# Opening in two half pieces with an identity made on the chip, and a last step that goes by token tiles

## The chip, the cores and the metric

The kernel runs on one core of a Trainium2 chip. The metric is device time in microseconds (us) of one execution; lower is better. TensorE is PE, VectorE is DVE, ScalarE is ACT, GpSimd is POOL, and SyncE (SP) issues most of the DMAs.

## The reference

One layer of a hybrid encoder in fp32, for one sequence of 256 tokens and a width of 2048:

```python
h = rms_norm(x, attn_norm[layer])
x = x + hybrid_mixer(h, w_in[layer], b_forget[layer], q_norm[layer], k_norm[layer],
                     out_norm_fox[layer], out_norm_sb[layer], w_out[layer])
h = rms_norm(x, ffn_norm[layer])
x = x + conv_ffn(h, w_up[layer], conv_w[layer], conv_b[layer], w_down[layer])
```

`hybrid_mixer` projects `h` with `w_in` (2048 x 6152) to queries, keys and values of 8 heads of forgetting attention, 8 forget gates, and queries, keys and values of 8 heads of stick-breaking attention; both results are normalized and go through `w_out` (2048 x 2048). `conv_ffn` is `w_up` (2048 x 11264), a causal convolution of width 3 per column, a SiLU gate, and `w_down` (5632 x 2048).

## The kernel before

The 256 tokens are two tiles of 128 (`NT`), the width is 16 tiles of 128 (`KT`). Nearly all of the time is products of the activations with the four weight matrices. Each weight is read once from DRAM, in pieces of up to 1 MB. For accuracy in fp32 each operand is split into a high and a low part: `split` (L238) lets ACT round a piece to `w_hi` (L242) and DVE subtract it from the raw piece to `w_lo` (L243), and `in_three` (L252) sums high x high, low x high and high x low in PSUM. The activations stand transposed in `hT` as a high and a low part.

The work is a list of steps, one per piece of weights. Each step has a load, perhaps a sum, a preparation (the split), products, and perhaps a follow-up. The loop at the end (L1242) writes them out staggered: step n's load stands six steps ahead of its products, its split two steps ahead. Every engine then runs its own instructions strictly in the order written. Loads go into five buffers in turn (`wraw`, L80), so a load waits until the piece five steps back has been split; high and low parts have three buffers each. SP issues the loads in order; some additions to weights and a reload of `x` go by POOL's DMA queue, for the first time long after the opening.

`opening` (L317) takes the first 688 columns of the values of `w_in`, for all 16 tiles of the width, in eight pieces of two tiles each (2 x 688 columns, 688 KB). `tokens` of a piece transposes two tiles of `x` on PE with an identity (`transposed`, L169, into `ps_x`), multiplies them by the norm's weight `ga` into `hT`, high part on ACT (L181) and low part on DVE (L182), and splits the piece. `matmuls` of a piece are 24 products of 128x344 into four banks `acc_v`; after them PE does the transposes of the piece two steps on. `ga` is a column form of `attn_norm`, which arrives as 16 rows in `prow` and is turned by a transpose of its own (`columns`, L164, into `pp`). The identity is the first 128 columns of `cst`, an input array of constants, and comes by DMA into `cs` (L327).

The order of SP's first transfers is: x tiles 0 and 1, identity, `attn_norm`, x tiles 2 and 3, weights 0, x tiles 4 and 5, weights 1, and so on. All other parameters are loaded behind the seventh piece (`load_parameters`, L138).

After the opening come the other projections (several with seven products instead of eight per block of four), the heads of attention in between, `w_out`, and the feed-forward. The last eight steps are `down_plain` (L1149) with `final` set: for each 512 output columns two pieces of 4 x 512 weights, 24 products of 128x512 each into the two halves of one tile `acc`, one half per token tile. Products of the two token tiles alternate. Then `added` (L1083) adds each half to `xb` on DVE (L1085) and sends it to `out` by SP (L1087).

Of the kernel before, what the change touches and what calls it, by code (L numbers as in the profile page):

```python
# [7 lines left out]

F32 = mybir.dt.float32
F32R = mybir.dt.float32r  # L10
AF = mybir.ActivationFunctionType
ALU = mybir.AluOpType
# [31 lines left out]
def hybrid_layer(  # L44
# [18 lines left out]
):  # L63
    nc = tc.nc
    act, dve = nc.scalar, nc.vector
    act.preload_act_table_set("natural_log_exp_and_others")

    xf = x.rearrange("b s d -> (b s) d")
    of = out.rearrange("b s d -> (b s) d")
# [20 lines left out]


    NC2 = 2 * NFT
    cs = const.tile([P, C_MF], F32, name="cs")
    prow = const.tile([50, P], F32, name="prow")
# [19 lines left out]
    def load_x(k, n, queue=nc.sync):  # L114
        queue.dma_start(x2[:, :, k * P : (k + n) * P], xp[:, :, k * P : (k + n) * P])

    ident = cs[:, C_ID : C_ID + P]
    tri = cs[:, C_TRI : C_TRI + P]
    tri_one = cs[:, C_TRI : C_TRI + 2 * P]
    ones = cs[:, C_ONE : C_ONE + P]  # L120
# [48 lines left out]
    def transposed(k):  # L169
        ps = psb.tile([P, 2, S], F32, name="ps_x", tag="t")  # L170
        for j in range(2):
            for t in range(NT):
                nc.tensor.transpose(  # L173
                    ps[:, j, t * P : (t + 1) * P], x2[:, t, (k + j) * P : (k + j + 1) * P], ident
                )
        return ps

    def split_tokens(ps, k, g):
        for j in range(2):
            i = k + j  # L180
            act.activation(hT[:, i, 0, :], ps[:, j, :], AF.Identity, scale=g[:, i : i + 1])  # L181
            dve.scalar_tensor_tensor(  # L182
                hT[:, i, 1, :], ps[:, j, :], g[:, i : i + 1], f32(hT[:, i, 0, :]),
                op0=ALU.mult, op1=ALU.subtract,
            )
# [19 lines left out]
    def new_step(load, sums, prepare, matmuls, follow=None):  # L205
        steps.append((load, sums, prepare, matmuls, follow))
# [31 lines left out]
    def split(raw, a, b):  # L238
        hi = whi.tile([P, 2048], F32R, name="w_hi", tag="w_hi")
        lo = wlo.tile([P, 2048], F32R, name="w_lo", tag="w_lo")  # L240
        n = a * b
        act.copy(hi[:, :n], raw[:, :n])  # L242
        dve.tensor_tensor(lo[:, :n], raw[:, :n], f32(hi[:, :n]), op=ALU.subtract)  # L243
# [8 lines left out]
    def in_three(accs, parts, n, lhs, starts, stops, cut=None, middle=None):  # L252

        hi, lo = parts
        order = [(i, l, hi) for i in range(n) for l in range(2)] + [(i, 0, lo) for i in range(n)]
        for j, (i, l, r) in enumerate(order):
            if middle and 2 * j == len(order):
                middle()
            for t, o in enumerate(accs):
                nc.tensor.matmul(  # L260
                    o, lhs(i, l, t), r[:, i, :] if cut is None else r[:, i, cut], start=starts and j == 0,
                    stop=stops and j == 3 * n - 1, skip_group_check=len(accs) == 1 and not starts,
                )

    def middle():
# [51 lines left out]
    def opening():  # L317

        banks = []
        x_loads = {0: [(4, 2)], 1: [(6, 2)], 2: [(8, 4)], 3: [(12, 4)]}  # L320
        mem = {}

        def piece(i):
            def loads():
                if i == 0:
                    load_x(0, 2)
                    nc.sync.dma_start(cs[:, :P], cst[:, :P])  # L327
                    nc.sync.dma_start(prow[:KT, :], attn_norm[0].rearrange("(n p) -> n p", p=P))
                    load_x(2, 2)
                mem["raw", i] = load(rows_of(wi, 2 * i, 2, V0, 2 * VC))  # L330
                for k, n in x_loads.get(i, ()):
                    load_x(k, n)
                if i == 6:
                    load_parameters()

            def tokens():
# [5 lines left out]
                if i % 2:  # L342
                    squares(ss1, i // 2)
                if i == 7:
                    ready.add("x")

            def matmuls():
                if i == 0:
                    banks.extend([bank_tile(f"acc_v{t}", 2 * j + t) for t in range(NT)] for j in range(2))
                for j in range(2):  # L350
                    in_three(
                        [banks[j][t][:, :VC] for t in range(NT)], mem["parts", i], 2, of_tokens(2 * i),
                        i == 0, i == 7, cut=slice(j * VC, (j + 1) * VC),
                    )
                if i + 2 < 8:
                    tokens_of[i + 2]()

            tokens_of.append(tokens)

            def follow():  # L360
                v = tile_of["v"] = at.tile([P, NT, WF], F32, name="vA", tag="v")
                for j in range(2):
                    for t in range(NT):
                        act.activation(
                            v[:, t, j * VC : (j + 1) * VC], banks[j][t][:, :VC], AF.Identity,
                            scale=rstd1[:, t : t + 1],
                        )
                    yield

            new_step(loads, None, tokens if i < 2 else None, matmuls, follow if i == 7 else None)  # L370

        tokens_of = []
        for i in range(8):
            piece(i)

    opening()


    def last_values():
# [703 lines left out]
    def added(c, ps, t, op=ALU.add, final=False):  # L1083
        xs = x2[:, t, c : c + 512]
        dve.tensor_tensor(xs, xs, ps, op=op)  # L1085
        if final:
            nc.sync.dma_start(of[t * P : (t + 1) * P, c : c + 512], xs)  # L1087
        yield
# [60 lines left out]
    def down_plain(part, c, final=False):  # L1149
        n = (part.f_hi - part.f_lo) // 4  # L1150
        cell = []

        def piece(kh):
            mem = {}

            def loads():
                mem["raw"] = load(rows_of(wd, part.f_lo + 4 * kh, 4, c, 512))

            def prepare():
                mem["parts"] = split(mem["raw"], 4, 512)  # L1160

            def matmuls():
                if kh == 0 and final:
# [4 lines left out]
                in_three(  # L1168
                    cell, mem["parts"], 4,
                    lambda i, p, t: of_half(part.pairs[2 * kh + i // 2][:, :, i % 2], p, t),  # L1170
                    kh == 0, kh == n - 1,
                )
# [56 lines left out]
    def begin(task):  # L1229
        next(task)  # L1230
        after.append(task)

    hooks[5] = lambda: following.append(factors1())
    hooks[7] = head_parameters
    hooks[13] = lambda: begin(token_sums())
# [82 lines left out]
```

## Time and profile before

| | us |
|---|---|
| median of three runs | 1116.45 (1116.01 to 1116.59) |
| the profiled execution, its own time | 1116.26 |
| span of the program in it (first to last instruction) | 1114.5 |
| PE busy | 1100.6 |
| DVE busy | 898.6 |
| ACT busy | 730.7 |
| first product of the opening starts | 10.36 |
| last product starts its row | 1107.46, with 8 products in 1.98 |

Times in the profile count from the start of the span. A row of the timeline has start and length in us, the engine, the line, the operation, what it writes and reads, shape and count, and in brackets how long the engine had been idle and what ended that. A row of a chain has start, length and name only. `xN` merges N instructions; lengths of products overlap, so N of them last less than N lengths. In groups, the numbers behind the bar are busy us and mean ns of one. Rows on DMAs have the count, KB each and the median us from issue to landing; POOLq and SPq are the queues of those who issue. The granted TensorE clock is 1.000 over the span.

### The profile page before, as it was taken

How to read it: one execution, taken by the hardware profiler on the slowest of the kernel's cores; microseconds unless marked ns; L12 is line 12 of the kernel's file. 1: busy time of each engine (PE TensorE's matmuls, PEld its weight loads, DVE VectorE, ACT ScalarE, POOL GpSimd, SP SyncE). 2: the span in 40 equal slices, each digit the busy share in tenths (PEclk: the TensorE clock that was granted, in tenths of full speed). 3: DMA queues.
4: the chain of work that ended last, by engine and by line, in shares of the span. 5: the costliest groups of instructions: out<-in, count | busy, mean ns of one | idle time of the engine just before them, and what ended most of it. 6: DMA issues, size and time to landing. Idle time of an engine off the chain costs nothing.

```text
span 1114.5 us, 14460 instructions
## 1 busy us (share of the span) xinstructions
PE 1100.6 (99%) x5730; PEld 948.7 (85%) x5730; DVE 898.6 (81%) x854; ACT 730.7 (66%) x915; POOL 36.6 (3%) x34
## 2 busy tenths in 40 slices
PE   7999999999999999999999999999999999999998
PEld 6988888888888888888888888888888888888886
DVE  4676888877897676666699898989899898999882
ACT  5645787667676467666676767776677666776751
POOL 0000000000100000000000000000000000000000
PEclk9999999999999999999999999999999999999999
DMA  8757877769778366555558796697958798597841
GB/s 290 268 197 209 242 189 249 184 199 259 262 174 281 114 197 200 191 190 192 190 150 242 233 262 228 189 283 197 276 182 213 261 239 274 152 289 202 265 159 66
DMA packets 166813, 240.75 MB, mean 216 GB/s; under 512 B 4168, under 2 KB 98010, under 8 KB 166746
## 3 DMA queue, kind: packets, MB, share of 16 engines
q1 hardware_dynamic: 152442, 210.47, 56.2%
q0 software_dynamic: 14304, 29.36, 15.0%
q8 instruction: 45, 0.74, 0.3%
q14 instruction: 22, 0.18, 0.0%
HBM read 237.72 MB, written 2.10 MB: 215 GB/s over the span
## 4 chain that ended last, share of the span: by engine, by line
PE 95%; DVE 2%; ACT 1%; issue 1%; DMA 1%; SPq 0%; DVEq 0%; ACTq 0%
PE pu L1069 44%; PE bank_a L260 16%; PE bank_b L260 8%; PE acc_o L260 5%; PE bank_c L260 4%; PE acc_v L260 4%; PE acc L260 4%; PE bank_p L260 4%; PE bank_e L260 2%; DVE w_lo L243 1%; ACT w_hi L242 1%; DMA w_raw<-in_w_in_dram 1%; PE ps_x L173 1%; PE ps_h L605 0%; PE ps_s L686 0%
## 5 line engine op out<-in xcount | busy, mean ns | idle before, releaser
L243 DVE TENSOR_TENSOR w_lo<-w_raw,w_hi 128x2048 fp32r<-128x2048 f32 (+1 forms) x239 | 537.2, 2252 | 146.1 <-ACT w_hi L242 145.5
L242 ACT CAST w_hi<-w_raw 128x2048 fp32r<-128x2048 f32 (+1 forms) x239 | 449.2, 1881 | 232.0 <-PE pu L1069 87.4
L1069 PE MATMUL pu<-hT,w_hi 128*128 128x512 f32 x1408 | 334.7, 390 | 0.0
L1069 PEld LDWEIGHTS pu<-hT,w_hi 128*128 128x128 f32 x1408 | 262.4, 188 | 53.4 <-DVE hT L182 0.3
L1069 PEld LDWEIGHTS pu<-hT,w_lo 128*128 128x128 f32 x1408 | 180.6, 191 | 6.9
L1069 PE MATMUL pu<-hT,w_lo 128*128 128x256 f32 x1408 | 182.8, 283 | 0.0
L999 ACT ACTIVATE tap<-up,ccol 128x256 f32<-128x256 f32 x176 | 74.6, 495 | 0.0
L260 PE MATMUL bank_a<-w_hi,g 128*128 128x512 f32 x192 | 47.3, 392 | 0.0
L1112 POOL DMA_DIRECT2D w_raw<-in_w_down_dram x16 | 20.5, 1282 | 687.9 <-DVE w_raw L1130 362.0
L260 PE MATMUL bank_a<-w_hi,hT 128*128 128x512 f32 x160 | 40.6, 396 | 0.0
L260 PEld LDWEIGHTS bank_a<-w_hi,g 128*128 128x128 f32 x192 | 34.8, 189 | 6.4
L260 PE MATMUL acc_v<-w_hi,hT 128*128 128x344 f32 x192 | 35.6, 333 | 2.9 <-ACT w_hi L242 2.9
L1130 DVE TENSOR_TENSOR w_raw<-w_raw 128x2048 f32<-128x2048 f32 x16 | 36.6, 2286 | 0.1
L260 PEld LDWEIGHTS acc_v<-w_hi,hT 128*128 128x128 f32 x192 | 31.9, 196 | 3.4 <-ACT w_hi L242 3.3
L260 PEld LDWEIGHTS bank_a<-w_hi,hT 128*128 128x128 f32 x160 | 29.2, 188 | 5.6
L1004 DVE TENSOR_TENSOR gate<-gate,tap 128x512 f32<-128x512 f32 x44 | 30.3, 688 | 2.7 <-DVE gate L1004 0.5
L1085 DVE TENSOR_TENSOR xb<-xb,bank_a 128x512 f32<-128x512 f32 x40 | 27.2, 680 | 6.2 <-PE bank_a L260 6.2
L1004 DVE TENSOR_TENSOR val<-val,tap 128x512 f32<-128x512 f32 x44 | 30.3, 688 | 2.3
L260 PE MATMUL bank_a<-w_hi,s 128*128 128x512 f32 x128 | 32.1, 392 | 0.0
L260 PE MATMUL bank_b<-w_hi,s 128*128 128x512 f32 x128 | 32.0, 392 | 0.0
L985 DVE TENSOR_TENSOR up<-t,R 128x512 f32<-128x512 f32 x44 | 30.4, 692 | 1.5
L260 PE MATMUL acc_o<-w_hi,oSb 128*128 128x512 f32 x128 | 31.3, 396 | 0.0
(273 smaller groups left out, 1410.7 us busy)
## 6 DMA issues: line engine op xcount, KB each, us to landing
w_raw<-in_w_up_dram SPq DMA_DIRECT2D x88, 1024.0 KB, 5.3
w_raw<-in_w_down_dram SPq DMA_DIRECT2D x44, 1024.0 KB, 5.2
w_raw<-in_w_in_dram SPq DMA_DIRECT2D x40, 1024.0 KB, 5.7
w_raw<-in_w_out_dram SPq DMA_DIRECT2D x16, 1024.0 KB, 6.3
w_raw<-in_w_down_dram POOLq DMA_DIRECT2D x16, 1024.0 KB, 8.9
w_raw<-in_w_in_dram SPq DMA_DIRECT2D x12, 688.0 KB, 8.1
w_raw<-in_w_in_dram POOLq DMA_DIRECT2D x8, 1024.0 KB, 9.7
xb<-in_x_dram POOLq DMA_DIRECT2D x4, 512.0 KB, 8.1
```

What stands on the lines that cost most here:

```text
L173: nc.tensor.transpose(ps[:, j, t * P : (t + 1) * P], x2[:, t, (k + j) * P : (k + j + 1) * P], ident)
L242: act.copy(hi[:, :n], raw[:, :n])
L243: dve.tensor_tensor(lo[:, :n], raw[:, :n], f32(hi[:, :n]), op=ALU.subtract)
L260: nc.tensor.matmul(o, lhs(i, l, t), r[:, i, :] if cut is None else r[:, i, cut], start=starts and j == 0, stop=stops and j == 3 * n - 1, s ...
L985: dve.tensor_tensor(u[:, :, 2:], t2, R, op=ALU.mult)
L999: act.activation(taps[w][:, j, :], u[:, j, w : w + S], AF.Copy, scale=ccol[:, w, f : f + 1])
L1004: dve.tensor_tensor(a, a, tap, op=ALU.add)
L1069: nc.tensor.matmul(acc[:, j, S:] if low else acc[:, j, :], (lo if low else hi)[:, i, j * P : (j + 1) * P], hT[:, k, 0, :] if low else hT[: ...
L1085: dve.tensor_tensor(xs, xs, ps, op=op)
L1112: nc.gpsimd.dma_start(mem[weights].rearrange("p (a b) -> p a b", a=4), plus, accum_op=ALU.add)
L1130: dve.tensor_tensor(mem[into], mem[a], mem[b], op=ALU.add)
```

## The change

It changes the two ends of the program and no product in between.

The opening has nine pieces, the first two of one tile each (344 KB). Piece 0 is rounded by DVE instead of ACT, and its products go high x high for all four banks, low x high, then high x low. Tiles 0 and 1 are transposed together ahead of piece 0, and the transposes of tiles 2 and 3 now stand between the products of piece 0 and piece 1; before, they stood ahead of all products. `attn_norm` is loaded by ACT's queue, ahead of ACT's table load. The identity is not loaded: `make_identity` has POOL write zeros and select ones on the diagonal. SP's order becomes x 0-1, weights 0, weights 1, x 2-3, weights 2, x 4-5, and so on. The hooks that follow the opening are counted from its end, so they keep their place.

The last step, which is the last 4 x 512 weights of the last 512 columns, goes by token tiles: 12 products of tile 0, its addition and transfer, 12 products of tile 1, whose addition and transfer are cut into two halves of 256 columns, one sent by SP and one by ACT. The two accumulators of these 512 columns are banks of their own.

```diff
-    act.preload_act_table_set("natural_log_exp_and_others")
...
+    prow = const.tile([50, P], F32, name="prow")
+    act.dma_start(prow[:KT, :], attn_norm[0].rearrange("(n p) -> n p", p=P))
+    act.preload_act_table_set("natural_log_exp_and_others")
...
     ident = cs[:, C_ID : C_ID + P]
+    make_identity(nc, ident)
...
-        x_loads = {0: [(4, 2)], 1: [(6, 2)], 2: [(8, 4)], 3: [(12, 4)]}
+        sizes = [1, 1] + [2] * 7
+        starts = [sum(sizes[:i]) for i in range(len(sizes))]
+        last = len(sizes) - 1
+        x_loads = {0: (0, 2), 1: (2, 2), 2: (4, 2), 3: (6, 2), 4: (8, 4), 5: (12, 4)}
...
             def loads():
                 if i == 0:
-                    load_x(0, 2)
-                    nc.sync.dma_start(cs[:, :P], cst[:, :P])
-                    nc.sync.dma_start(prow[:KT, :], attn_norm[0].rearrange("(n p) -> n p", p=P))
-                    load_x(2, 2)
-                mem["raw", i] = load(rows_of(wi, 2 * i, 2, V0, 2 * VC))
-                for k, n in x_loads.get(i, ()):
-                    load_x(k, n)
-                if i == 6:
+                    load_x(*x_loads[i])
+                mem["raw", i] = load(rows_of(wi, k0, n, V0, 2 * VC))
+                if 0 < i < 6:
+                    load_x(*x_loads[i])
+                if i == 7:
                     load_parameters()
 
             def tokens():
-                ps = transposed(2 * i)
-                if i == 0:
+                if n == 1 and i == 0:
                     columns(ga, prow[:KT, :], KT)
-                split_tokens(ps, 2 * i, ga)
-                mem["parts", i] = split(mem["raw", i], 2, 2 * VC)
+                    ps = mem["ps"] = transposed(0)
+                    hi, lo = cast(mem["raw", 0], 2 * VC, dve.tensor_copy)
+                    split_tokens(ps, 0, ga, 1)
+                    mem["parts", 0] = subtracted(mem["raw", 0], hi, lo, 1, 2 * VC)
+                elif n == 1:
+                    split_tokens(mem["ps"], 0, ga, 1, 1)
+                    mem["parts", 1] = split(mem["raw", 1], 1, 2 * VC)
+                else:
+                    split_tokens(transposed(k0), k0, ga)
+                    mem["parts", i] = split(mem["raw", i], 2, 2 * VC)
...
+                if final and kh == n - 1 and c == D - 512:
+                    for t in range(NT):
+                        in_three([cell[t]], mem["parts"], 4, lambda i, p, _: lhs(i, p, t), kh == 0, True, group=True)
+                        if t < NT - 1:
+                            for _ in added(c, cell[t], t, final=True):
+                                pass
...
             def follow():
+                if final and c == D - 512:
+                    for h, queue in enumerate((nc.sync, act)):
+                        cut = slice(h * 256, (h + 1) * 256)
+                        xs = x2[:, NT - 1, c + h * 256 : c + (h + 1) * 256]
+                        dve.tensor_tensor(xs, xs, cell[NT - 1][:, cut], op=ALU.add)
+                        queue.dma_start(of[(NT - 1) * P :, c + h * 256 : c + (h + 1) * 256], xs)
+                    return
```

How the instructions stand on the engines shows three places. The first is POOL, from the start of the program. Before, its own work begins with a DMA (the first row of weights is far behind the opening):

```order
L1303 ISA
L1303 MEMSET const-float32-0.0 128x1
L1303 MEMSET const-float32-1.0 128x1
L1303 MEMSET const-bfloat16-1.0 128x1
L1303 MEMSET const-uint8-127 128x1
L1313 UNCONDITIONAL_BRANCH
L489 DMA w_raw<-in_w_in_dram 128x4x512 x8
```

With the change, `cs` being the constants' tile whose first 128 columns are the identity:

```order
L1345 MEMSET const-uint8-127 128x1
L1355 UNCONDITIONAL_BRANCH
masks.py:197 MEMSET cs 128x128
masks.py:199 ISA
masks.py:199 AFFINE_SELECT cs<-cs 128x128
L518 DMA w_raw<-in_w_in_dram 128x4x512 x8
```

Three instructions are new ahead of POOL's first DMA. [...]

The second place is PE at the start, before:

```order
L173 MATMUL ps_x<-cs,xa 128x128 x4
L166 MATMUL pp<-cs,prow 128x16
L173 MATMUL ps_x<-cs,xa 128x128 x4
L260 MATMUL acc_v_184<-w_hi,hT 128x344
L260 MATMUL acc_v_185<-w_hi,hT 128x344
```

and with the change, where L373 are the products of a half piece and `acc_v_168` to `acc_v_171` the four banks:

```order
L169 MATMUL pp<-cs,prow 128x16
L176 MATMUL ps_x<-cs,xa 128x128 x4
L373 MATMUL acc_v_168<-w_hi,hT 128x344
L373 MATMUL acc_v_169<-w_hi,hT 128x344
...
L373 MATMUL acc_v_171<-w_lo,hT 128x344
L176 MATMUL ps_x<-cs,xa 128x128 x4
L373 MATMUL acc_v_168<-w_hi,hT 128x344
```

The transpose of `prow` (`pp`) moved to the front, where it is what waits for the identity; the second four transposes moved from ahead of all products to behind the first twelve. On DVE the rows `COPY ga<-pp` and then `CAST w_hi<-w_raw 128x688` are the first two with the change.

The third place is PE at the end. `bank_a_8927` and `bank_a_8928` are the accumulators of token tiles 0 and 1 in the changed kernel, the two names with `g2` the activations:

```order
L269 MATMUL bank_a_8927<-w_hi_8923,g2_8526 128x512 x4
L269 MATMUL bank_a_8927<-w_hi_8923,g2_8782 128x512 x4
L269 MATMUL bank_a_8927<-w_lo_8924,g2_8526 128x512 x2
L269 MATMUL bank_a_8927<-w_lo_8924,g2_8782 128x512 x2
L269 MATMUL bank_a_8928<-w_hi_8923,g2_8526 128x512 x4
L269 MATMUL bank_a_8928<-w_hi_8923,g2_8782 128x512 x4
L269 MATMUL bank_a_8928<-w_lo_8924,g2_8526 128x512 x2
L269 MATMUL bank_a_8928<-w_lo_8924,g2_8782 128x512 x2
```

Before, the last four rows of products are 8, 8, 4 and 4 into one `acc`, with the two tiles in turn. Now tile 0 is complete 12 products ahead of the end.

More of the change, by code (lines that the diff above doesn't have):

```diff
@@ L7 @@
 from concourse._compat import with_exitstack
+from concourse.masks import make_identity
 F32 = mybir.dt.float32
@@ L176, in transposed, with split_tokens @@
         return ps
-    def split_tokens(ps, k, g):
-        for j in range(2):
+    def split_tokens(ps, k, g, n=2, j0=0):
+        for j in range(j0, j0 + n):
             i = k + j
@@ L236, in load, with cast, split, subtracted @@
         return raw
-    def split(raw, a, b):
+    def cast(raw, n, copy):
         hi = whi.tile([P, 2048], F32R, name="w_hi", tag="w_hi")
         lo = wlo.tile([P, 2048], F32R, name="w_lo", tag="w_lo")
+        copy(hi[:, :n], raw[:, :n])
+        return hi, lo
+    def split(raw, a, b):
+        return subtracted(raw, *cast(raw, a * b, act.copy), a, b)
+    def subtracted(raw, hi, lo, a, b):
         n = a * b
-        act.copy(hi[:, :n], raw[:, :n])
         dve.tensor_tensor(lo[:, :n], raw[:, :n], f32(hi[:, :n]), op=ALU.subtract)
@@ L250, in rows_of, with in_three @@
         return w[k0 * P : (k0 + n) * P, c0 : c0 + cols].rearrange("(k p) c -> p k c", p=P)
-    def in_three(accs, parts, n, lhs, starts, stops, cut=None, middle=None):
+    def in_three(accs, parts, n, lhs, starts, stops, cut=None, middle=None, group=False):
         hi, lo = parts
@@ L261, in in_three @@
                     o, lhs(i, l, t), r[:, i, :] if cut is None else r[:, i, cut], start=starts and j == 0,
-                    stop=stops and j == 3 * n - 1, skip_group_check=len(accs) == 1 and not starts,
+                    stop=stops and j == 3 * n - 1, skip_group_check=len(accs) == 1 and not starts and not group,
                 )
@@ L349, in matmuls @@
                     banks.extend([bank_tile(f"acc_v{t}", 2 * j + t) for t in range(NT)] for j in range(2))
[L350 to L355, printed above, removed]
+                if n == 1:
+                    hi, lo = mem["parts", i]
+                    for l, w in ((0, hi), (1, hi), (0, lo)):
+                        for j in range(2):
+                            for t in range(NT):
+                                nc.tensor.matmul(
+                                    banks[j][t][:, :VC], of_half(hT[:, k0], l, t),
+                                    w[:, 0, j * VC : (j + 1) * VC], start=i == l == 0 and w is hi, stop=False,
+                                )
+                else:
+                    for j in range(2):
+                        in_three(
+                            [banks[j][t][:, :VC] for t in range(NT)], mem["parts", i], 2, of_tokens(k0),
+                            False, i == last, cut=slice(j * VC, (j + 1) * VC),
+                        )
+                if i + 2 <= last:
                     tokens_of[i + 2]()
@@ L368, in follow @@
                     yield
-            new_step(loads, None, tokens if i < 2 else None, matmuls, follow if i == 7 else None)
+            new_step(loads, None, tokens if i < 2 else None, matmuls, follow if i == last else None)
         tokens_of = []
-        for i in range(8):
+        for i in range(len(sizes)):
             piece(i)
     opening()
+    V_END = len(steps)
     def last_values():
@@ L1162, in matmuls @@
             def matmuls():
-                if kh == 0 and final:
+                if kh == 0 and final and c < D - 512:
                     acc = acc_tile("acc")
@@ L1167, in matmuls, with lhs @@
                     cell.extend(psb.tile([P, 512], F32, name="bank_a", tag="t") for _ in range(NT))
[L1168 to L1172, printed above, removed]
-            def follow():
+                def lhs(i, p, t):
+                    return of_half(part.pairs[2 * kh + i // 2][:, :, i % 2], p, t)
+                if final and kh == n - 1 and c == D - 512:
+                    for t in range(NT):
+                        in_three([cell[t]], mem["parts"], 4, lambda i, p, _: lhs(i, p, t), kh == 0, True, group=True)
+                        if t < NT - 1:
+                            for _ in added(c, cell[t], t, final=True):
+                                pass
+                else:
+                    in_three(cell, mem["parts"], 4, lhs, kh == 0, kh == n - 1)
+            def follow():
+                if final and c == D - 512:
[5 more added lines that the diff above has]
+                    return
                 for t in range(NT):
@@ L1231, in begin @@
         after.append(task)
[L1233 to L1235 removed]
+    hooks[V_END - 3] = lambda: following.append(factors1())
+    hooks[V_END - 1] = head_parameters
+    hooks[V_END + 5] = lambda: begin(token_sums())
     hooks[D_UNIT + 7] = reload_x
```

8 lines of the change are left out of this document (4 added, 4 removed).

## The prediction

> **What bounds the kernel now.** I read the page first, for the share of the engines and the chain that ended last.
>
> ```profile
> span 1114.5 us, 14460 instructions
> PE 1100.6 (99%) x5730; PEld 948.7 (85%) x5730; DVE 898.6 (81%) x854; ACT 730.7 (66%) x915; POOL 36.6 (3%) x34
> PE 95%; DVE 2%; ACT 1%; issue 1%; DMA 1%; SPq 0%; DVEq 0%; ACTq 0%
> ```
>
> TensorE is busy for 99% of the span and carries 95% of the chain. The change leaves every product of the middle as it is, so only the time before PE runs without a break, and the time after its last product, can move. Hence the second view: the chain in order of time, at its start.
>
> ```profile
> 2.67 6.28 DMA w_raw<-in_w_in_dram
> 8.95 0.02 issue
> 8.97 1.35 ACT w_hi L242
> 10.36 5.97 PE acc_v L260 x24
> 16.34 0.44 PE ps_x L173 x4
> 16.77 3.80 PE acc_v L260 x24
> ```
>
> The first piece of weights lands at 8.95, ACT rounds it, and PE starts at 10.36. Its first 24 products take 5.97 us, every later 24 take 3.80: PE starts at a lower pace. From there PE never waits in this stretch, so whatever moves PE's continuous start moves the end by as much. The third view is the timeline around that start and one later piece.
>
> ```profile
> 0.34 0.10 POOL L1303 MEMSET const-uint8-127<- 128x1 uint8 x1
> 0.73 1.28 ACT L66 ACT_TABLE_LOAD   x1 [0.73 <-PEq L1303]
> 0.74 0.44 SPq L115 DMA_DIRECT2D xa<-in_x_dram  x1
> ...
> 4.12 1.08 PE L173 MATMUL ps_x<-cs,xa 128*128 128x128 f32 x4 [4.12 <-DMA cs<-in_cst_dram]
> 5.13 0.28 PE L166 MATMUL pp<-cs,prow 16*128 16x16 f32 x1
> 5.45 0.17 DVE L167 COPY ga<-pp 128x16 f32<-128x16 f32 x1 [5.45 <-PE pp L166]
> 5.66 0.48 ACT L181 ACTIVATE hT<-ps_x,ga 128x256 fp32r<-128x256 f32 x1 [3.64 <-DVE ga L167]
> 6.30 1.11 PE L173 MATMUL ps_x<-cs,xa 128*128 128x128 f32 x4 [0.88 <-DMA xa<-in_x_dram]
> 12.82 1.35 PE L260 MATMUL acc_v<-w_lo,hT 128*128 128x344 f32 x4
> 13.96 1.73 PE L260 MATMUL acc_v<-w_hi,hT 128*128 128x344 f32 x8
> 16.53 1.51 PE L260 MATMUL acc_v<-w_hi,hT 128*128 128x344 f32 x8
> 16.81 0.47 ACT L181 ACTIVATE hT<-ps_x,ga 128x256 fp32r<-128x256 f32 x1 [1.37 <-PE ps_x L173]
> 17.32 0.48 DVE L182 SCALAR_TENSOR_TENSOR hT<-ps_x,ga,hT 128x256 fp32r<-128x256 f32 x1 [1.63 <-ACT hT L181]
> 17.84 0.47 ACT L181 ACTIVATE hT<-ps_x,ga 128x256 fp32r<-128x256 f32 x1 [0.55 <-DVE hT L182]
> 18.21 1.33 ACT L242 CAST w_hi<-w_raw 128x1376 fp32r<-128x1376 f32 x1
> 19.57 1.59 DVE L243 TENSOR_TENSOR w_lo<-w_raw,w_hi 128x1376 fp32r<-128x1376 f32 x1 [0.75 <-ACT w_hi L242]
> ```
>
> The reader sees here: the first transposes wait for the identity that a DMA brings and run at 4.12; four early products take 13.96 - 12.82 = 1.14 us (0.285 each), later ones 3.80 / 24 = 0.158; and the work from the last transpose of a piece to its `w_hi` is 16.81 to 19.54, 2.73 us.
>
> **The identity.** Now POOL makes it: a memset, an instruction that the built program names PseudoReloadLibraryIndex (GpSimd loads its library of routines), and the affine select. PE's first instruction waits for all three, and everything of the opening stands behind it: the norm's column `ga`, the first transposes, and on DVE, behind `ga`, even the cast of the first weights. Call t0 the time at which PE gets the identity.
>
> POOL is free at 0.75 (SP's row at 0.74 is where the engines enter). For memset and select of 128x128 I take 0.2 and 0.3, worked up from POOL's 0.10 for a memset of 128x1 and DVE's 0.22 for 128x128 (L1218 below); signalling is 0.1. So t0 = 1.35 + L, L being the load. No row shows such a load. Below stands zero (nothing to fetch), then ACT's load of its own table, 1.28 us; above stand the transfers that POOL itself starts:
>
> ```profile
> w_raw<-in_w_up_dram SPq DMA_DIRECT2D x88, 1024.0 KB, 5.3
> w_raw<-in_w_down_dram POOLq DMA_DIRECT2D x16, 1024.0 KB, 8.9
> w_raw<-in_w_in_dram SPq DMA_DIRECT2D x12, 688.0 KB, 8.1
> w_raw<-in_w_in_dram POOLq DMA_DIRECT2D x8, 1024.0 KB, 9.7
> ```
>
> I take L = 8.9, the median of POOL's largest group: it is POOL that fetches, from the same DRAM, and it does so while the opening's loads saturate the DMA engines (those of the opening need 8.1). That makes t0 = 10.25, later than the 4.1 at which the DMA brings the identity today, and as late as PE's present start.
>
> [...]
>
> **The opening from t0 on.** `pp` 0.28, copy of `ga` 0.17: t0+0.5. The four transposes behind `pp` end at t0+1.2 (1.11 in their row). ACT makes the high part of the first tile in 0.48: t0+1.7, and PE starts its products. DVE's cast of 128x688 fits between (0.5, scaled up from the rows of 128x128 and 128x512 below), with `w_lo` of that half piece (half of 1.59) ready before its eight high products are through.
>
> ```profile
> L1218 DVE CAST identR<-cs 128x128 fp32r<-128x128 f32 x1 | 0.2, 218 | 0.0
> L1219 DVE CAST masksR<-masks 128x512 fp32r<-128x512 f32 x1 | 0.4, 420 | 0.0
> L691 DVE TENSOR_TENSOR ps_s<-ps_s,masksR 128x256 f32<-128x256 f32 x8 | 3.4, 426 | 0.3 <-PE ps_s L688 0.2
> ```
>
> Twelve products at the early pace: 12 x 0.285 = 3.4, t0+5.1. Then the transposes of tiles 2 and 3, at that pace too, 0.44 x 0.285 / 0.158 = 0.8 to issue: t0+5.9; their results come 0.3 later (the row of 1.11), t0+6.2. The early pace ends today inside the row at 13.96, which is 0.3 longer than eight products later are, so near 14.6, 4.3 us behind the first product; I let it last as long, to t0+6.0. Piece 1: 12 x 0.158 = 1.9, t0+7.8; next transposes 0.44, t0+8.3. But piece 2's `w_hi` needs 2.73 us from t0+6.2, so it is there at t0+9.0: **a new wait of 0.7**, since a half piece of 1.9 us no longer covers the preparation that a whole piece of 3.80 did. Its low part (1.59) comes at t0+10.6, when the eight high products (1.3) are done at t0+10.3: another 0.3. Counted in, piece 2 starts as if at t0+9.4. The same products (tiles 2 and 3) start at 16.53 today. Thereafter the pieces are the same; ACT's squarings in every second piece follow its cast and find room in the 4.2 us (3.80 + 0.44) of a piece.
>
> So the opening gains 16.53 - 9.4 - t0 = 7.1 - t0. With t0 = 10.25 it **loses 3.1**.
>
> **What is covered.** `attn_norm` on ACT's queue puts about 0.45 of issue ahead of the table load, which then ends near 2.5; ACT's first work is after t0. SP drops two issues ahead of the weights (0.9); with a late identity nothing waits for those weights. The sixth weight load waits for DVE's `w_lo` of piece 0 (five buffers), at t0+3.1; SP's later loads queue behind it, but ten earlier loads keep the DMA busy until then. POOL's next work in the trace is a DMA at 99.88. The ninth piece adds no product: 12 + 12 replace 24. The parameters' loads keep their place ahead of the last piece. If cover were gone there, the cost would be a late piece of 688 KB, some 2 us at 390 GB/s.
>
> **The tail.**
>
> ```profile
> 1083.27 27.85 SPq L1087 DMA_DIRECT2D out_dram<-xb  x8
> 1107.46 1.98 PE L260 MATMUL acc<-w_lo,g 128*128 128x512 f32 x8
> 1109.48 1.28 DVE L1085 TENSOR_TENSOR xb<-xb,acc 128x512 f32<-128x512 f32 x2 [4.16 <-PE acc L260]
> out_dram<-xb SPq DMA_DIRECT2D x4, 256.0 KB, 2.4
> ```
>
> Today DVE adds both token tiles after the last product, until 1110.76, and the last 256 KB are issued then and land 2.4 us later. After: tile 0 is added and sent while PE works on tile 1; then two half adds of 0.43 (the 128x256 row of L691), overlapping by 0.08 as today's two do: done 0.5 us earlier. The last transfer is 128 KB, 0 to 0.35 us shorter (at the 390 GB/s of the window below), on ACT's queue, which is empty. I take a **gain of 0.7** (0.5 to 0.85). PE's products are the same in number.
>
> **Sum.** Change = L + 1.35 - 7.1 - 0.7 = L - 6.5, about +2.4 us on the profiled execution, whose own time is 1116.26 (span 1114.5 plus 1.8 around). The median of the three runs is 1116.45, 0.2 above. Predicted: **1118.8**. Two tenths of a per cent, 2.2 us, is about what a measurement of this kernel can tell from no change; the forecast stands on that edge, which decides how I split the chances.
>
> **Rivals.** *Faster: the library is already there* (L under 3). Then data decide:
>
> ```profile
> 0.00:4.00 4.00, 0.00 (x0) 0.00 (x0) 0.00 (x0) 1.28 (x1) 0.20 (x4) 1.00 0.39 112
> 4.00:8.00 4.00, 2.41 (x9) 1.60 (x9) 1.14 (x3) 0.95 (x2) 0.00 (x0) 1.00 0.94 291
> 16.00:20.00 4.00, 4.00 (x29) 3.99 (x28) 1.39 (x3) 2.18 (x3) 0.00 (x0) 1.00 1.04 390
> ```
>
> The last two columns are the DMA share and GB/s: 448 KB have moved by 4.0, then 291 a microsecond. The first weights stand 600 KB deep in SP's queue instead of 1272, so they are through at 4.5 instead of 6.8; the present ones landed 2.1 after that, so 4.5 to 6.6. PE's products start at 5.7 to 6.8 (t0+1.7), t0 is in effect 4.0 to 5.1, the opening gains 2.0 to 3.1, and with the tail the time is 1112.7 to 1113.9. For it: before runs its first POOL work with no such load. Against: the program does ask for the load, ahead of the select. It decides if t0 is under 5.6. Chance 0.28.
>
> *No change: a load as quick as an undisturbed transfer.* L = 5.3, the row of `w_up`: t0 = 6.65, opening +0.45, tail 0.7, time 1115.3; up to L = 6.9 at 1116.9. Against it: the opening's transfers take 8.1. Chance 0.13. [...]
>
> *Much slower: the load shares the DMA engines unfairly,* one part behind each of the stream's transfers: twice POOL's 9.7, 19.4, gives +13, about 1129. The stream runs at 390 GB/s, which speaks for it; against it, POOL's transfers take no more than 1.7 times SP's of the same size (8.9 to 5.3). Chance 0.07.
>
> **How the numbers follow.** The forecast, L of 6.9 to 11, has 0.52 and its own range 1116.9 to 1121.0; of it I count 0.19 within 0.2% (L under 8.7) and 0.33 beyond. Faster by over 0.2%: 0.28. Within: 0.13 + 0.19 = 0.32. Slower: 0.33 + 0.07 = 0.40. The range takes in the first rival and the forecast: 1112.6 to 1121.2, and leaves out the long load and some edges, under 0.2.
>
> **What would show it.** In the profile of the changed kernel: PE's first row (`pp`) waits for POOL's affine select, near 10; a gap on POOL between memset and select as long as L; the first weights landed long before PE starts, and DVE's cast of them behind `ga`; PE idle about 0.7 us ahead of piece 2; last adds of 128x256 and two transfers at the end, issued about 0.5 us sooner. The forecast is wrong if `pp` runs before 5 (then the first rival), and the pipeline's step if piece 2 starts other than 9.4 us behind `pp`.

## The result, and the profile after

The changed kernel takes **1111.88 us** (1111.54 to 1112.66) where the kernel before, in the same comparison, takes 1116.52 (1116.01 to 1116.80). The ratio is 0.9961, with an interval of 0.9949 to 0.9973. It became 4.6 us faster, where 2.4 slower was forecast. The profiled execution took 1111.54 with a span of 1109.8; what lies around the span is 1.8, as before, so the whole difference (4.72) lies in the span.

The page of the changed kernel, its span, engines and shares of the chain:

```profile
span 1109.8 us, 14472 instructions
PE 1099.7 (99%) x5730; PEld 948.4 (85%) x5730; DVE 899.3 (81%) x857; ACT 730.0 (66%) x915; POOL 37.1 (3%) x36
PE 95%; DVE 3%; ACT 1%; issue 1%; DMA 0%; SPq 0%; DVEq 0%; ACTq 0%
```

PE's busy time is 0.9 less than before, for the same 5730 instructions; the other 3.8 are time in which PE no longer stands idle. The chain in order of time, at its start:

```profile
1.24 3.85 DMA w_raw<-in_w_in_dram
...
5.11 0.53 DVE w_hi L244
...
5.78 3.43 PE acc_v L373 x12
9.21 0.45 PE ps_x L176 x4
...
11.08 1.34 ACT w_hi L244
...
12.44 1.60 DVE w_lo L252
...
14.09 2.78 PE acc_v L269 x16
...
17.31 3.80 PE acc_v L269 x24
```

As before, the chain begins with a load of weights, now a half piece that lands at 5.09 instead of 8.95. GpSimd does not appear in it. New are the links from 9.21 to 14.09: PE waits for ACT and DVE to prepare the third piece. From 17.31 on the steps are those of before (24 products in 3.80). The timeline of the same stretch:

```profile
0.74 0.20 POOL masks.py:197 MEMSET cs<- 128x128 f32 x1 [0.29 <-POOLq L1345]
1.02 0.29 POOL masks.py:199 TENSOR_SCALAR_AFFINE_SELECT cs<-cs 128x128 f32<-128x128 f32 x1
3.48 0.25 PE L169 MATMUL pp<-cs,prow 16*128 16x16 f32 x1 [3.48 <-DMA prow<-in_attn_norm_dram]
3.88 1.12 PE L176 MATMUL ps_x<-cs,xa 128*128 128x128 f32 x4 [0.15 <-DMA xa<-in_x_dram]
5.78 2.63 PE L373 MATMUL acc_v<-w_hi,hT 128*128 128x344 f32 x8 [0.78 <-DVE w_hi L244]
8.21 0.99 PE L373 MATMUL acc_v<-w_lo,hT 128*128 128x344 f32 x4
9.04 0.60 PE L176 MATMUL ps_x<-cs,xa 128*128 128x128 f32 x4
12.46 1.24 PEld L269 LDWEIGHTS acc_v<-w_hi,hT 128*128 128x128 f32 x8 [0.74 <-ACT w_hi L244]
12.46 1.52 PE L269 MATMUL acc_v<-w_hi,hT 128*128 128x344 f32 x8 [0.50 <-ACT w_hi L244]
14.09 0.62 PEld L269 LDWEIGHTS acc_v<-w_lo,hT 128*128 128x128 f32 x4 [0.39 <-DVE w_lo L252]
17.06 1.51 PE L269 MATMUL acc_v<-w_hi,hT 128*128 128x344 f32 x8
```

POOL's memset ends at 0.94 and the affine select starts at 1.02. Between them stands the instruction that the built program names PseudoReloadLibraryIndex, here called the request for the library, and 0.08 us is all it can have cost by these rows. That it loads a library is read from its name alone; nothing in the rows shows that anything was loaded. The identity is ready at 1.31, and `pp` waits for `attn_norm` instead, until 3.48. PEld, in two of the rows, is PE's loading of weights, which starts ahead of the products (for the four low ones of piece 0 at 7.93, the products at 8.21). Counted there, the wait for piece 2 is 0.74; in the products' own row it is 0.50, since the transposes ahead of them run on until 11.97. The row at 17.06 has the products of tiles 4 and 5, which stood here in the kernel before:

```profile
20.77 1.50 PE L260 MATMUL acc_v<-w_hi,hT 128*128 128x344 f32 x8
```

The opening gained 3.71. The last product ends at 1105.68 where it ended at 1109.44, 3.76 earlier: nothing of it is given back in between. The rest is the tail, in which token tile 0 is added while PE works on tile 1:

```profile
1103.00 0.69 DVE L1114 TENSOR_TENSOR xb<-xb,bank_a 128x512 f32<-128x512 f32 x1 [1.44 <-PE bank_a L269]
1105.72 0.75 DVE L1214 TENSOR_TENSOR xb<-xb,bank_a 128x256 f32<-128x256 f32 x2 [2.03 <-PE bank_a L269]
1106.17 0.33 SPq L1215 DMA_DIRECT2D out_dram<-xb  x1
1106.50 0.38 ACTq L1215 DMA_DIRECT2D out_dram<-xb  x1
```

The last issue of the kernel before came 1.35 behind its last product, here it is 0.82:

```profile
1110.79 0.33 SPq L1087 DMA_DIRECT2D out_dram<-xb  x1
```

From the end of the last product to the end of the span it is 4.09 now (1109.77 - 1105.68) and was 5.05: 0.97 less, taken before rounding. 3.76 and 0.97 are the 4.72, to rounding.

### The profile page after: what moved, and what is told of

Read it like the earlier page. It is cut to its first block, busy times and chain, and to the rows that moved or that the text cites. A ratio compares the mean times of both kernels' runs of the same rounds, so it can differ in the third digit from the quotient of the medians.

```text
span 1109.8 us, 14472 instructions
## 1 busy us (share of the span) xinstructions
PE 1099.7 (99%) x5730; PEld 948.4 (85%) x5730; DVE 899.3 (81%) x857; ACT 730.0 (66%) x915; POOL 37.1 (3%) x36
## 4 chain that ended last, share of the span: by engine, by line
PE 95%; DVE 3%; ACT 1%; issue 1%; DMA 0%; SPq 0%; DVEq 0%; ACTq 0%
PE pu L1098 44%; PE bank_a L269 17%; PE bank_b L269 8%; PE acc_o L269 5%; PE bank_c L269 4%; PE bank_p L269 4%; PE acc_v L269 4%; PE acc L269 3%; PE bank_e L269 2%; DVE w_lo L252 1%; ACT w_hi L244 1%; PE ps_x L176 1%; PE ps_h L634 0%; DMA w_raw<-in_w_in_dram 0%; PE ps_s L715 0%
## 5 line engine op out<-in xcount | busy, mean ns | idle before, releaser
L252 DVE TENSOR_TENSOR w_lo<-w_raw,w_hi 128x2048 fp32r<-128x2048 f32 (+2 forms) x240 | 537.4, 2244 | 143.0 <-ACT w_hi L244 142.3
L244 ACT CAST w_hi<-w_raw 128x2048 fp32r<-128x2048 f32 (+2 forms) x239 | 448.7, 1878 | 229.4 <-PE pu L1098 92.3
L269 PE MATMUL bank_a<-w_hi,g 128*128 128x512 f32 x224 | 55.1, 392 | 0.0
L269 PEld LDWEIGHTS bank_a<-w_hi,g 128*128 128x128 f32 x224 | 40.8, 189 | 7.6
L269 PE MATMUL acc_v<-w_hi,hT 128*128 128x344 f32 x176 | 31.2, 323 | 0.5 <-ACT w_hi L244 0.5
L269 PE MATMUL bank_p<-w_hi,hT 128*128 128x512 f32 x128 | 30.5, 391 | 0.0
```

The costliest lines, as they stand in the source:

```text
L269: nc.tensor.matmul(o, lhs(i, l, t), r[:, i, :] if cut is None else r[:, i, cut], start=starts and j == 0, stop=stops and j == 3 * n - 1, s ...
```

## The experiments

Each kernel was timed beside the kernel before, whose median was 1116.41, 1115.95 and 1116.28 in the three sets (e1 to e4, e5 to e8, e9 to e11). Behind a time stand its ratio to the kernel before and the interval of that ratio. The intervals of e1, e3 and e6 to e8 overlap that of the changed kernel, so their differences of medians from it are only as good as the starts in the traces that are given with them. Theory one was then: the request for the library costs nothing, and the first weights, 600 KB deep in SP's queue instead of 1272, set the start. The rivals were that the identity's way, or the half pieces, had done it.

### Does a request for a library cost anything? (e5)

```diff
+    nc.gpsimd.memset(cs, 0.0)
+    nc.gpsimd.partition_broadcast(cs[:, :P], cs[0:1, P : 2 * P])
     make_identity(nc, ident)
```

> The changed kernel with one more GpSimd operation ahead of the identity: a broadcast of one row of cs over the partitions (its result is overwritten later), whose routine is in another library than the affine select, so that the program asks for library 1 where it asked for 0. Theory 'resident' (the request costs nothing in the changed kernel only because GpSimd already holds library 0): POOL stands still for several us between its first memset and the broadcast, the affine select ends at 8 to 12.5, pp waits for it, and by the line measured with the late identity (1108 + t0, t0 = start of pp) the time is 1116 to 1120.5. Theory 'always quick' (a load of any library costs under a microsecond here): POOL is through before 3.5, pp stays near 3.5 behind prow's DMA, and the time is that of the changed kernel, 1111.3 to 1112.7.

POOL in its timeline:

```profile
0.74 0.43 POOL L120 MEMSET cs<- 128x398 f32 x1 [0.29 <-POOLq L1347]
1.31 0.42 POOL L121 PARTITION_BROADCAST cs<-cs  x1
1.80 0.20 POOL masks.py:197 MEMSET cs<- 128x128 f32 x1
2.08 0.29 POOL masks.py:199 TENSOR_SCALAR_AFFINE_SELECT cs<-cs 128x128 f32<-128x128 f32 x1
```

The gap with the request is 0.14 (1.17 to 1.31), `pp` starts at 3.54, and the time is 1112.2 (0.9966, 0.9954 to 0.9979). "Always quick" holds, for this other library too. Nor does the profile count a fetch that goes with the request. These are the instruction queues of the changed kernel (packets, MB, share of the DMA engines):

```profile
q8 instruction: 45, 0.74, 0.3%
q14 instruction: 23, 0.18, 0.0%
```

The kernel before had 45 and 22 packets there; e5 has 45 and 22, and so have e4 and e8, which make the same request as the changed kernel. The one packet more is thus not the request's. Whether both libraries lie on the chip anyway or are brought in before the span starts, no run here tells.

### What if the identity did come late? (e4)

```diff
+    for _ in range(20):
+        nc.gpsimd.memset(cs, 0.0)
     make_identity(nc, ident)
```

> The changed kernel with POOL held up by 20 memsets of 128x398 ahead of the identity (0.3 to 0.45 us each), so that PE gets it at t0 of about 7 to 10, as the prediction had assumed for a load of the library. It tests the prediction's steps behind t0. By them the first product starts at t0+1.7, piece 2 at t0+9.0 with 0.3 to 0.4 of waiting for its low part, and the opening gains 7.1 - t0; since the early pace ended 2.8 us behind the first product in the changed kernel and not 4.3, the constant may come out up to 0.7 higher. With t0 = 9: the opening loses 1.2 to 1.9, the last step gains 0.97, the time is 1116.8 to 1117.5. If the steps were wrong as well (the rival: a late start lets later work catch up, because the loads are there), the loss is under half of t0's delay.

Its timeline, POOL and PE:

```profile
0.74 9.71 POOL L121 MEMSET cs<- 128x398 f32 x20 [0.29 <-POOLq L1347]
10.79 0.29 POOL masks.py:199 TENSOR_SCALAR_AFFINE_SELECT cs<-cs 128x128 f32<-128x128 f32 x1
11.13 0.28 PE L171 MATMUL pp<-cs,prow 16*128 16x16 f32 x1 [11.13 <-POOL cs masks.py:199]
19.86 1.24 PEld L271 LDWEIGHTS acc_v<-w_hi,hT 128*128 128x128 f32 x8 [0.74 <-ACT w_hi L246]
21.49 0.61 PEld L271 LDWEIGHTS acc_v<-w_lo,hT 128*128 128x128 f32 x4 [0.38 <-DVE w_lo L254]
```

1119.58 (1.0027, 1.0017 to 1.0037): slower than before, by 3.2; the prediction's L - 6.5 gives 3.3 for this t0 (L = 11.13 - 1.35). t0 came 2.13 later than the 9 of the expectation, which moved by as much is 1118.9 to 1119.6. With t0 = 11.13 the same products as above start at 24.46, a loss of 3.69, where 7.1 - t0 gives 4.0. So the prediction's steps behind t0 stand, and had the load cost what it assumed, its forecast would have come about.

### The identity by DMA (e1)

```diff
-    make_identity(nc, ident)
...
                 if i == 0:
                     load_x(*x_loads[i])
+                    nc.sync.dma_start(cs[:, :P], cst[:, :P])
```

> The changed kernel, but the identity comes by DMA again, on SP's queue behind x tiles 0 and 1 and ahead of the first half piece of weights; attn_norm stays on ACT's queue. Theory 'queue' (the gain of the opening comes from the first weights standing 600 instead of 1272 KB deep in SP's queue and being half a piece): the 64 KB of the identity push the weights back by 0.2 to 0.4 us and the identity lands at about 4.1 instead of being there at 1.3, so PE's first product starts at 6.0 to 6.3 instead of 5.78; the time is 0.2 to 0.5 us above the changed kernel's 1111.9, at 1112.1 to 1112.4. Theory 'identity' (the identity's own DMA was what held the opening): most of the opening's 3.75 us are lost again, 1114 to 1115.6.

1113.16 (0.997, 0.9959 to 0.9981), 1.28 above the changed kernel: between the two theories, and in the range of neither. Its PE and its cast:

```profile
4.22 0.25 PE L167 MATMUL pp<-cs,prow 16*128 16x16 f32 x1 [4.22 <-DMA cs<-in_cst_dram]
6.05 0.52 DVE L242 CAST w_hi<-w_raw 128x688 fp32r<-128x688 f32 x1 [1.37 <-DMA w_raw<-in_w_in_dram]
6.72 2.63 PE L372 MATMUL acc_v<-w_hi,hT 128*128 128x344 f32 x8 [1.20 <-DVE w_hi L242]
11.01 2.02 PE L372 MATMUL acc_v<-w_hi,hT 128*128 128x344 f32 x8
```

`pp` waits for the identity, and the weights land 0.94 later than in the changed kernel (6.03 for 5.09). DVE's cast still waits for the weights, so what decides is when the weights land, and not the wait for the identity. Of the 0.94, 0.50 is that SP issues them later (1.74 for 1.24); the 64 KB ahead of them are 0.2 at the prediction's 291 KB a microsecond, and the rest is open. In e6, whose loads are those of the changed kernel, the weights landed at 5.45, so 0.4 can lie between two executions. The first product starts 0.94 later; a longer early pace (below) does the rest in this execution, in which tiles 4 and 5 start at 18.78, 1.72 later.

### Half pieces, and the wait that they bring (e3, e6)

```diff
-        sizes = [1, 1] + [2] * 7
+        sizes = [2] * 8
```

In e3, x tiles 2 and 3 stand directly behind the first weights, and ACT rounds the first piece; identity, queues and tail stay as changed.

> The changed kernel with eight whole pieces of two tiles again, the first one split by ACT as before, and with x tiles 2 and 3 behind the first weights; the identity on the chip, attn_norm on ACT's queue and the last step are kept. Theory 'queue': the first weights stand 944 KB deep and land near 6.0; the transposes of tiles 2 and 3, which here precede all products, wait for x near 7.3; ACT's cast of a whole piece (1.33) ends near 7.8; PE's products start at 8.0 to 8.5, and no wait follows them. Since a start at 10.36 gave 16.53 for tiles 2 and 3, this gives 14.2 to 14.7, against 12.46 plus waits of 0.4 in the changed kernel: 1.3 to 1.9 us above it, 1113.2 to 1113.8. If half pieces cost with their waits what they win (the rival), it is level with the changed kernel.

1112.9 (0.9969, 0.9957 to 0.9981), 1.0 above the changed kernel; 1.3 was the least expected. The first products start at 8.00, 2.2 later, right behind the transposes of tiles 2 and 3, which here wait for `x` until 7.23; PE does not wait again. The products of tiles 4 and 5 start at 18.27, 1.2 behind the changed kernel: half pieces start 2.2 earlier and give 1.0 of it back in this trace, the two waits of piece 2 (0.74 and 0.39) among it. Some 0.5 of the 1.2 is an early pace that in e3 was 1.15 longer (4.10 for 2.95).

In e6 the transposes of tiles 2 and 3 move up, between the eight high and four low products of piece 0:

```diff
                     for l, w in ((0, hi), (1, hi), (0, lo)):
+                        if i == 0 and w is lo:
+                            tokens_of[2]()
...
-                if i + 2 <= last:
+                if 0 < i <= last - 2:
                     tokens_of[i + 2]()
```

> The changed kernel with the transposes of tiles 2 and 3 (and ACT's and DVE's work behind them) between piece 0's eight high and four low products instead of behind all twelve. Theory 'half piece too short' (the new wait ahead of piece 2 is there because 12 products do not cover the preparation): w_hi of piece 2 comes about 0.6 us earlier, the 0.74 us wait ahead of its products falls to 0 to 0.2, the 0.39 ahead of its low products may stay; 0.5 to 0.9 us less than the changed kernel, 1111.0 to 1111.4. Rival 'the data' (piece 2's weights or x tiles land too late for it): the wait stays and the time is within 0.3 of the changed kernel.

1111.69 (0.9961, 0.9949 to 0.9974): 0.2 better by the medians, and the ratio is that of the changed kernel, so the expected gain of 0.5 to 0.9 is missed. PE:

```profile
8.56 1.06 PE L176 MATMUL ps_x<-cs,xa 128*128 128x128 f32 x4
9.27 1.50 PE L375 MATMUL acc_v<-w_lo,hT 128*128 128x344 f32 x4
10.56 1.70 PE L375 MATMUL acc_v<-w_hi,hT 128*128 128x344 f32 x8
13.08 1.51 PE L269 MATMUL acc_v<-w_hi,hT 128*128 128x344 f32 x8
```

Both waits are gone, yet piece 2 starts at 13.08. In this execution the first product started at 6.13 (0.35 later), PE was at its early pace (0.29 from one product to the next, see below) until about 11.1, not 8.7, and work at that pace filled the time in which it would have waited. That made the early pace the next thing to test.

### The tail alone (e2)

The kernel before with the change of the last step only.

> The kernel before with the last step of the change alone. Both traces put the last product 3.75 us earlier and the end of the span 4.72 us earlier, so the last step should be worth 0.97 us by itself: 1115.5. By the prediction's term of 0.5 to 0.85 it would be 1115.7 to 1116.0. If the two ends of the program interact (the rival), it is worth under 0.3 us.

1115.37 (0.9992, 0.9983 to 1.0), 1.04 below the kernel before; from the last product to the end 4.09 where it was 5.05. That is as expected. The interval reaches 1.0, so it is the trace that shows it.

Taken singly, the identity on the chip is worth 1.3 by the medians, the half pieces 1.0 and the tail 1.0, of 4.6 together. What is left, with `attn_norm` on ACT's queue and `x` tiles 2 and 3 behind two pieces of weights in it, was not run alone.

### The early pace (e7, e8, e11, and again e9, e10)

Read from the single products, the step from one to the next is 0.29 at first and 0.16 later. The change-over comes 4.39 us behind the first product in the kernel before, 2.95 in the changed one, and 5.52, 5.25, 4.10, 3.27, 2.95 and 5.00 in e1 to e6. It differs where the opening is the same: e2 has that of the kernel before, with 5.25 for 4.39. The window view of the changed kernel, whose third column from the right is the granted clock, shows none of it (1.00 in both stretches):

```profile
0.00:4.00 4.00, 0.37 (x2) 0.30 (x3) 0.17 (x1) 1.28 (x1) 0.69 (x6) 1.00 0.50 123
4.00:8.00 4.00, 3.22 (x12) 2.85 (x13) 2.87 (x5) 1.60 (x3) 0.00 (x0) 1.00 1.00 340
```

A microsecond of it costs 0.45 (1 - 0.158 / 0.287) where PE would not have waited anyway. e7 gives PE products of zeros in its idle time, which nothing reads:

```diff
+    dve.memset(junk[:, :P], 0.0)
+
+    def warm(n):
+        wt = psb.tile([P, 512], F32, name="warm", tag="t")
+        for _ in range(n):
+            nc.tensor.matmul(wt[:, :P], junk[:, :P], junk[:, :P], start=True, stop=True)
+
+    warm(5)
...
                     ps = mem["ps"] = transposed(0)
+                    warm(2)
```

> The changed kernel with five products of zeros (128x128, plain fp32) on PE ahead of pp, from about 1.2 to 3.4, and two behind the first transposes, in PE's idle time. Theory 'PE needs some microseconds of work before it goes at full pace': the early pace, which lasted 2.95 to 5.5 us behind the first product, ends 1 to 3 us after it; every microsecond less is worth 0.445 in products, of which the waits for piece 2 take back up to 1.0 us; time 0.3 to 1 us below the changed kernel, 1110.9 to 1111.6. Rival 'the pace goes by a clock of its own, whatever PE did before': the early pace again ends at any point in 2.95 to 5.5, and the time is within 0.6 of the changed kernel on either side.

```profile
1.06 2.50 PE L126 MATMUL warm<-junk 128*128 128x128 f32 x10 [1.06 <-DVE junk L121]
4.72 0.61 PE L126 MATMUL warm<-junk 128*128 128x128 f32 x4
5.76 1.52 PE L382 MATMUL acc_v<-w_hi,hT 128*128 128x344 f32 x8 [0.43 <-DVE w_hi L252]
11.75 1.53 PE L277 MATMUL acc_v<-w_hi,hT 128*128 128x344 f32 x8 [0.32 <-ACT w_hi L252]
```

The first eight products take 1.52 instead of 2.63. 1110.94 (0.9957, 0.9945 to 0.9970): 0.9 below the changed kernel by the median, but PE now waits for `x` (0.40) and for piece 2 (0.32). Of the five executions three took 1110.41 to 1110.94 and two 1112.08 and 1112.33, which is no gain; only the one of 1110.94 has a profile. So e7 alone does not settle it. e8 joins e6 and e7:

> Both: early transposes of tiles 2 and 3, and the seven products of zeros. If both theories hold, the gains add, since the earlier preparation takes away the wait that the quicker products would run into: 1.2 to 2 us below the changed kernel, 1109.9 to 1110.7. If only the first holds, about 1111.2; if neither, 1111.9.

1110.16 (0.9948, 0.9934 to 0.9961), as expected if both theories hold. Its tiles 4 and 5 start at 15.46, 1.6 ahead of the changed kernel. e9, the changed kernel, and e10, the kernel of e8, were then run side by side:

> The changed kernel once more, beside the next two: 1111.3 to 1112.7, and an early pace of any length between 2.9 and 5.5 us behind the first product.

> Early transposes and products of zeros together, once more, for the direct comparison with the changed kernel: 1.4 to 2.0 us below it, 1109.9 to 1110.5, with an early pace of under 1.5 us behind the first product.

1112.28 (0.9962, 0.9948 to 0.9975) and 1110.18 (0.9945, 0.9932 to 0.9957): 2.10 between them, a little over what was expected, and every execution of e10 was quicker than every one of e9. This version beats both kernels of the case. e9's early pace lasted 6.14, longer than expected; in its PE rows the second half piece falls under it too, and the wait of 0.74 is absent:

```profile
5.78 2.63 PE L373 MATMUL acc_v<-w_hi,hT 128*128 128x344 f32 x8 [0.76 <-DVE w_hi L244]
...
10.06 2.35 PE L373 MATMUL acc_v<-w_hi,hT 128*128 128x344 f32 x8
13.24 1.05 PE L269 MATMUL acc_v<-w_hi,hT 128*128 128x344 f32 x5
```

Last, the kernel before with nothing but such products: two behind `pp`, six behind the second transposes.

```diff
                     columns(ga, prow[:KT, :], KT)
+                    warm(2)
+                if i == 1:
+                    warm(6)
```

> The kernel before with products of zeros alone (two behind pp, six behind the transposes of tiles 2 and 3), in the time in which PE waits for the first weights. Theory 'PE needs some microseconds of nearly unbroken work before it goes at full pace': the early pace, 4.39 us behind the first product in the kernel before, ends by 1.5 us behind it; the first 24 products take 4.0 to 4.7 instead of 5.97, nothing behind them waits (a whole piece covers the preparation), and the time is 1.2 to 1.9 us below the kernel before. Rival 'the pace goes by a clock of its own': within 0.6 of the kernel before.

1114.58 (0.9985, 0.9976 to 0.9994), 1.70 below the kernel before, as expected; the slowest of its executions (1114.96) was quicker than the quickest of the kernel before (1115.27). In its chain the first 24 products take 4.43 instead of 5.97:

```profile
10.34 4.43 PE acc_v L267 x24
...
15.20 3.80 PE acc_v L267 x24
```

In e8 and e11 the early pace ended 0.72 and 0.39 behind the first product, and in e7 and e10 ahead of it: in e7 the second zeros, at 4.72, already take 0.61 (above), where in e8 they took 1.06:

```profile
4.85 1.06 PE L126 MATMUL warm<-junk 128*128 128x128 f32 x4
```

In the nine profiles without zeros it ended 2.95 to 6.14 behind the first product. So PE's own earlier work moved the change-over in these runs, and no count from the start of the program gives it: it came at 10.7 in e11, at 14.75 in the kernel before.

## Why the prediction was wrong

**The step that failed is the load of GpSimd's library**, "I take L = 8.9, the median of POOL's largest group". The gap holding the request is 0.08, and 0.14 for another library. The range of the unknown reached down to zero, rightly; the choice inside it was wrong. The row that I took times megabytes of weights and says nothing of a library; that both are issued by GpSimd was no likeness. No run shows the term L: that there is a load at all was read from the instruction's name, and what the runs show in its place are the gaps of 0.08 and 0.14. The error is some 8.8 us in this one term. With L near zero the line L - 6.5 no longer holds, since then the identity is not what is late: the first rival takes over, as written ("it decides if t0 is under 5.6").

**The rival was right in mechanism and a little small.** It put the first weights at 4.5 to 6.6 and the products at 5.7 to 6.8; they came at 5.09 and 5.78. (Its upper ends do not fit each other: weights at 6.6 and the prediction's cast of 0.5 make 7.1, not 6.8.) Its time was 1112.7 to 1113.9, measured 1111.88. Two sizes make the difference. The effective t0 is 5.78 - 1.7 = 4.08, for which 7.1 - t0 gives 3.0, and the opening gained 3.71: this execution's early pace was 1.44 shorter than that of before (2.95 for 4.39), worth 0.64. With 6.14, in e9, the same products start at 17.84, a gain of 2.9. And the tail gained 0.97 instead of 0.7: the last issue came 0.53 sooner behind the last product, as predicted 0.5, and its 128 KB took 3.27 from issue to the end of the span where 256 KB took 3.70, 0.43 less where 0 to 0.35 was allowed.

**The new wait was right:** 0.7 and 0.3 predicted, 0.74 and 0.39 measured in the rows of PEld, and the same in e4 (0.74 and 0.38). It is there only if the early pace ends early enough, so part of the agreement is luck: the prediction took 4.3 us for the early pace and this execution had 2.95; with 5.52 in e1 the first wait was 0.33, with 6.14 in e9 it was absent.

**The steps behind t0 were right** (e4: first product at t0 + 1.90 for 1.7, `w_hi` of piece 2 at t0 + 8.7 for 9.0, which with the second wait counted in is 9.1 for the 9.4 that the prediction gave as its sign, POOL's own two operations 0.20 and 0.29 as estimated, and 0.05 from the end of the select to `pp` where the prediction put 0.1 for signalling). What was "covered" was covered: the gain at 17.06 arrives at the last product unchanged.

## What to carry to other kernels

An operation that no trace shows is best bounded from both sides and then tested in one short run by itself, ahead of any forecast that hangs on it; the nearest row by engine need not be a likeness in kind. In an opening, count what stands in the queue up to the first operand: with 600 KB instead of 1272, and three issues fewer ahead of it, the first weights landed at 5.09 instead of 8.95. Of these 3.86, 1.43 is the earlier issue (1.24 for 2.67); how the rest divides between fewer bytes ahead and a piece of half the size was not run. Where TensorE idled ahead of its first products here, 7 or 8 products of zeros in that time ended the early pace ahead of the first product or at most 0.72 behind it, which was worth 1.7 us in the kernel before and 1.7 to 2.1 in the changed one together with earlier transposes; without these it was 0.9 by the median, and nothing in two executions of five. And a shorter first piece gives back the part of the next one's preparation that it no longer covers (0.74 and 0.39 here).

## What was not expected of the hardware

The early pace lasted between 2.95 and 6.14 us behind the first product, 3.2 of difference, and the same program (the changed kernel and e9) had both ends. At 0.45 a microsecond this is 1.4 us of a run, partly hidden where PE would have waited anyway; the executions of the changed kernel differ by 1.1 (1111.54 to 1112.66). The granted clock reads 1.00 in both rows of the window view of the changed kernel, and 1.0 as the mean over the span of e9.

In e7 the change-over came 3.7 us behind the first product of zeros (4.72 for 1.06); in e8, with the same zeros, it came 5.4 behind it (6.50 for 1.06).
